# The second half's last five transposed column pairs computed as seven products for eight

## The chip, the cores and the metric

The kernel runs on one core of a Trainium2 chip. The metric is the device time of one execution in microseconds. Before the change it is 1893.95 us, the median of 3 runs (1892.88 to 1894.11).

## What is computed

One layer of a streaming encoder on 2048 prompt frames and 64 sample frames of width 1024:

```
h = rmsnorm(x, norm_g) @ w_in                  # 1024 -> 6144 columns
qa, ka, va, za, qb, kb, vb, zb, ga, gb = split(h)
oa = differential attention of qa, ka, va      # block-causal, 4 heads
ob = retention of qb, kb, vb                   # chunks of 64 frames, 4 heads
m  = sigmoid(ga) * ((norm(oa) * silu(za)) @ w_o_diff) + sigmoid(gb) * ((norm(ob) * silu(zb)) @ w_o_ret)
y  = x + m @ w_out
```

The outputs also hold the keys, the values and the retention state.

## The kernel before, in words

**Precision.** Every fp32 operand of a large product is split into two fp32r parts, high and low, and a product takes three matmuls: high by high, high by low, low by high. So each product appears in the profile as `xh,wh`, `xl,wh`, `xh,wl` (or with the weights first).

**Halves.** The frames are worked in two halves: frames 0 to 1023, and frames 1024 to 2047 with the 64 sample frames, 1088 in all. In each half the columns of `w_in` come as wide blocks of 512 (va, ka, qa, vb, by `natural`), which need row layout, and as 16 pairs of 2 x 128 columns (qb, kb, za, zb: two pairs each; ga, gb: four each), which are wanted transposed, columns on the partitions and frames on the free dimension.

**The 16 pairs of half 0** use a scheme of Strassen's kind (`strassen`, matmuls on L889): the 1024 inner columns are cut in two, the 256 output columns in two and the frames in two, and 7 products of sums of such blocks stand for the 8 plain products. The sums of the weights are made by POOL in `sum_prep` (operands b11, b21, b22 are plain blocks, t1 to t4 are sums), the sums of x once for all pairs.

**The 16 pairs of half 1** use the plain product (`transposed`, L1329, matmuls in `mm_group`, L1039): for each of the two column halves, the frames come in groups of 512, 256 and 320, and a group is 8 inner blocks x 3 matmuls. ACT copies each group out of its bank (`fin_t`, L1356 and L1358) into an `ev` buffer, from which it is stored to DRAM (zaT, zbT, gaT, gbT). The weights come by DMA (`ws`), ACT makes the high part (`wh`, L993) and POOL the low one (`wl`, L1003).

**Order.** An event loop in Python (`loop`) runs tasks by priority with a cost model and so writes the order of PE, ACT and DVE, which is kept as written. The order of SP, which issues all DMAs, and of POOL is made by the framework's scheduler. The attention over a half (`attn_head`, scores on L1577 and L1578, transposes on L1689, values on L1667 to L1669) and the retention run in one stream of tasks, `z_stream`; the products of the columns in another, `w_stream`, of lower priority, which fills PE while attention waits for the softmax. For the second half attention starts in the last group of the first transposed pair of half 1 and ends before the last pairs, so the last stretch of `w_stream` is pure products. Then `out_stream` reads za, zb, ga, gb and the attention results back (`z`, `on`, `ga`, `gb`), multiplies by w_o (`m_tile`, L2367 to L2369, 264 frames at a time) and by w_out (`y_quad`, L2491 to L2493).

A DMA on SP waits until the one issued eight before it has landed; SP works its list strictly in order.

## Time and profile before

| what | us |
|---|---|
| median of the runs | 1893.95 |
| the profiled execution | 1895.42 |
| its span in the profile | 1893.5 |
| PE busy | 1878.8 (99%) |
| DVE busy | 1267.1 (67%) |
| ACT busy | 955.2 (50%) |
| POOL busy | 586.2 (31%) |

The profiled execution is 1.9 us longer than its span, the time before the first and after the last instruction. The digits by slices of the profile's page are for 40 slices of 47.3 us. PE's busy time of a group of matmuls sums their durations, which overlap, since a matmul starts before the one ahead has ended; what a matmul costs is the distance from its start to the next start, read from the timeline. The waits of PE add up to under 10 us.

### The profile page before, as it was taken

How to read it: one execution, taken by the hardware profiler on the slowest of the kernel's cores; microseconds unless marked ns; L12 is line 12 of the kernel's file. 1: busy time of each engine (PE TensorE's matmuls, PEld its weight loads, DVE VectorE, ACT ScalarE, POOL GpSimd, SP SyncE). 2: the span in 40 equal slices, each digit the busy share in tenths (PEclk: the TensorE clock that was granted, in tenths of full speed). 3: DMA queues.
4: the chain of work that ended last, by engine and by line, in shares of the span. 5: the costliest groups of instructions: out<-in, count | busy, mean ns of one | idle time of the engine just before them, and what ended most of it. 6: DMA issues, size and time to landing. Idle time of an engine off the chain costs nothing.

```text
span 1893.5 us, 32104 instructions
## 1 busy us (share of the span) xinstructions
PE 1878.8 (99%) x10970; PEld 1649.9 (87%) x10970; DVE 1267.1 (67%) x2994; ACT 955.2 (50%) x2217; POOL 586.2 (31%) x557
## 2 busy tenths in 40 slices
PE   9999999999999999999999999999999999999999
PEld 7788888888888789888888899999999999999887
DVE  6765856657565667877577567668685339977664
ACT  6444654454434566465556454555565536654221
POOL 2420355555643132031211301211202535512442
PEclk9999999999999999999999999999999999999999
DMA  7664555565666885464524633643512758876542
GB/s 255 213 175 124 168 166 169 173 185 182 180 181 180 239 230 159 137 207 131 162 72 112 187 99 114 154 115 94 139 55 74 230 173 263 270 235 211 168 156 78
DMA packets 360581, 313.01 MB, mean 165 GB/s; under 512 B 67937, under 2 KB 310241, under 8 KB 360418
## 3 DMA queue, kind: packets, MB, share of 16 engines
q1 hardware_dynamic: 360418, 310.97, 55.8%
q8 instruction: 86, 1.41, 0.3%
q14 instruction: 77, 0.63, 0.1%
HBM read 205.43 MB, written 104.60 MB: 164 GB/s over the span
## 4 chain that ended last, share of the span: by engine, by line
PE 65%; DMA 1%; DVE 1%; SPq 1%; ACT 0%; issue 0%; ACTq 0%; POOL 0%; DVEq 0%; POOLq 0%
PE mm L1039 27%; PE at L1689 3%; PE s L1577 2%; PE s L1578 2%; PE pv L1669 2%; PE pv L1668 2%; PE pv L1667 2%; PE s L2491 1%; PE s L2493 1%; PE s L2492 1%; PE at L2368 1%; PE s L2368 1%; PE mm L2367 1%; PE s L2367 1%; PE at L2367 1%; PE s L2369 1%
## 5 line engine op out<-in xcount | busy, mean ns | idle before, releaser
L1003 POOL TENSOR_TENSOR wl<-ws,wh 128x512 fp32r<-128x512 f32 x125 | 167.7, 1355 | 384.3 <-ACT wh L993 309.8
L1039 PE MATMUL mm<-xh,wh 128*128 128x256 f32 (+2 forms) x784 | 259.7, 331 | 0.0
L1039 PE MATMUL mm<-xh,wl 128*128 128x256 f32 (+2 forms) x784 | 254.4, 325 | 1.5 <-POOL wl L1003 1.5
L1039 PE MATMUL mm<-xl,wh 128*128 128x256 f32 (+2 forms) x784 | 254.2, 324 | 0.0
L1039 PE MATMUL mm<-wh,xh 128*128 128x512 f32 x504 | 203.6, 404 | 0.0
L1039 PE MATMUL mm<-wh,xl 128*128 128x512 f32 x504 | 198.3, 393 | 0.0
L1039 PE MATMUL mm<-wl,xh 128*128 128x512 f32 x504 | 197.9, 393 | 0.0
L1617 ACT ACTIVATE row<-row,a_mx 128x1024 f32<-128x1024 f32 (+7 forms) x144 | 149.8, 1043 | 19.6 <-DVE a_mx L1596 19.5
L1039 PEld LDWEIGHTS mm<-xh,wl 128*128 128x128 f32 x784 | 148.0, 189 | 11.9 <-POOL wl L1003 1.9
L1039 PEld LDWEIGHTS mm<-xl,wh 128*128 128x128 f32 x784 | 148.4, 189 | 9.8
L1039 PEld LDWEIGHTS mm<-xh,wh 128*128 128x128 f32 x784 | 148.2, 189 | 10.0
L1705 DVE TENSOR_TENSOR atl<-at,ath 128x512 fp32r<-128x512 f32 (+1 forms) x144 | 92.8, 659 | 90.4 <-ACT ath L1703 90.1
L1703 ACT CAST ath<-at 128x512 fp32r<-128x512 f32 (+1 forms) x144 | 79.4, 565 | 116.6 <-PE at L1689 111.3
L1448 POOL TENSOR_TENSOR r_y<-r_y,r_sq 128x256 f32<-128x256 f32 x32 | 30.1, 941 | 340.6 <-DVE r_sq L1445 160.1
L1586 DVE CUSTOM_DVE_ANT_0 row<-s,dfar 128x512 f32<-128x512 f32 (+2 forms) x146 | 90.5, 634 | 60.2 <-PE s L1578 55.6
L768 POOL TENSOR_TENSOR wl<-ws,wh 128x256 fp32r<-128x256 f32 x64 | 57.8, 903 | 196.0 <-ACT wh L759 190.8
L1039 PEld LDWEIGHTS mm<-wh,xl 128*128 128x128 f32 x504 | 94.8, 188 | 21.4
L1039 PEld LDWEIGHTS mm<-wh,xh 128*128 128x128 f32 x504 | 95.1, 189 | 17.3 <-DVE raw L1211 0.2
L1039 PEld LDWEIGHTS mm<-wl,xh 128*128 128x128 f32 x504 | 95.2, 189 | 17.0
L1639 DVE SCALAR_TENSOR_TENSOR row<-row,a_w 128x1024 f32<-128x1024 f32 (+5 forms) x88 | 98.1, 1124 | 0.0
L1577 PE MATMUL s<-K,q 128*128 128x512 f32 (+3 forms) x244 | 91.6, 378 | 0.4 <-DVE a_acc L1586 0.2
L993 ACT CAST wh<-ws 128x512 fp32r<-128x512 f32 x128 | 77.5, 621 | 28.2 <-DMA ws<-in_w_in_dram 16.3
(497 smaller groups left out, 5442.0 us busy)
## 6 DMA issues: line engine op xcount, KB each, us to landing
ws<-in_w_in_dram SPq DMA_DIRECT2D x160, 256.0 KB, 3.4
q<-qT SPq DMA_DIRECT2D x128, 128.0 KB, 3.5
K<-kT SPq DMA_DIRECT2D x48, 256.0 KB, 4.2
V<-vN SPq DMA_DIRECT2D x24, 512.0 KB, 5.2
row<-in_x_prompt_dram SPq DMA_DIRECT2D x16, 512.0 KB, 4.3
wz<-in_w_in_dram SPq DMA_DIRECT2D x32, 256.0 KB, 4.0
row<-in_cache_k_T_dram SPq DMA_DIRECT2D x32, 256.0 KB, 3.6
row<-in_cache_v_diff_dram SPq DMA_DIRECT2D x32, 256.0 KB, 3.2
```

Source lines behind the costliest of these rows:

```text
L768: nc.gpsimd.tensor_sub(l[:, cs], src, h[:, cs].bitcast(F32))
L993: self.nc.scalar.copy(h, st)
L1003: self.nc.gpsimd.tensor_sub(l, st, h.bitcast(F32))
L1039: nc.tensor.matmul(ps, p, q, start=c == 0 and i == 0, stop=c == KC - 1 and i == 2)
L1577: nc.tensor.matmul(ps, q1s, kk, start=True, stop=False)
L1586: nc.vector.tensor_tensor_reduce(out=row[:, k0:k0 + n], in0=ps, in1=tab, scale=-SLOPES[h], scalar=3.0e38, op0=ALU.add, op1=ALU.min, accum_ ...
L1617: nc.scalar.activation(u, u, AF.Exp, bias=mx, scale=-1.0, accum_out=lp[:, k:k + 1])
L1639: nc.vector.scalar_tensor_tensor(out=u0, in0=u1, scalar=w[:, 0:1], in1=u0, op0=ALU.mult, op1=ALU.add)
L1689: nc.tensor.transpose(at[:, w:w + 128], src, self.ident)
L1703: nc.scalar.copy(ah[:, :w], at[:, :w])
L1705: nc.vector.tensor_sub(al[:, :w], at[:, :w], ah[:, :w].bitcast(F32))
L2367: nc.tensor.matmul(ps, wh[:, u, csl], oh, start=kt == 0, stop=False)
```

## The change

The first 11 pairs of half 1 stay plain products, with the frames in groups of 512, 288 and 288 (the 64 sample frames are split in two times 32). The last 5 pairs (the last of ga and all four of gb) go to a new function `quad`: 7 products of sums for 8, in the order of `PHASES`, product by product over all 5 pairs. A product of one pair is a group of 256 and a group of 288 frames, each of 4 inner blocks x 3 matmuls (L1547).

- **x operands.** The seven x operands (three plain blocks, four sums) are written to DRAM (`xd`) after the natural blocks of half 1: 12 stores of plain blocks straight from the x tiles, and 20 chunks of sums, each 8 adds on POOL, a cast on ACT, a subtraction on DVE and two stores (`x_again`, `x_chunk`). `x_pass` reads each phase's operand back, 2 x 1.114 MB (128 x 2176, high and low), into one of two slots in the x tile of the second 576 frames, after the last plain pair has read it.
- **Weight operands.** In half 0, `sum_keep` stores the sums t1 to t4 of the last 5 pairs to DRAM (`wsum`, 20 stores of 256 KB); in half 1, each product of a pair loads one 128 x 4 x 128 operand, from `wsum` or from `w_in`. Between load and matmul stand the cast on ACT and the subtraction on POOL or DVE (`next_low`).
- **Evacuation.** The banks of `quad` are added to running sums by DVE (`q_scaled`), with an ACT copy for two products of the seven; finished blocks go to `ev` and are stored in pieces of 128 x 256, and the sample frames 128 x 4 x 8.
- **Attention.** `attn_head` waits for its head's keys only; `at_pv` waits for the values.
- The x tiles of half 1 are laid out by block of frames, the weight sum t4 is formed earlier in the pair.

```diff
+PLAIN = 11
+PHASES = [("t2", "S2", "q_p6"), ("b11", "A11", "q_p1"), ("b21", "A12", "q_p2"), ("t1", "S1", "q_p5"),
+          ("t3", "S3", "q_p7"), ("t4", "A22", "q_p4"), ("b22", "S4", "q_p3")]
+NAMES = ("S1", "S3", "S2", "S4", "A11", "A12", "A22")
+WIDTH = (256, 288)
...
+        else:
+            for name, *_ in PHASES:
+                k = ("t1", "t2", "t4", "t3", "b11", "b21", "b22").index(name)
+                for c in c0:
+                    if k < 4:
+                        src = self.wsum[self.wpair[c], k // 2, :, :, 128 * (k % 2):128 * (k % 2) + 128]
+                    else:
+                        r0, n0 = ((0, 0), (512, 0), (512, 128))[k - 4]
+                        src = w[r0:r0 + 512, c + n0:c + n0 + 128].rearrange("(c p) n -> p c n", p=128)
+                    yield [128, 4, 128], src
...
+    def next_low(self, st, h, l, t, new, kind):
+        yield t - LAT
+        eng, cost = self.lighter() if kind == "quad" else (self.nc.gpsimd, self.G)
+        eng.tensor_sub(l, st, h.bitcast(F32))
+        t = cost(512, t)
+        self.give("ws", t)
...
+    def sum_keep(self, pair, i, k, raw, left, t):
+        yield t
+        b1, b2, tt = raw[i][0]
+        src = b1 if k else tt
+        t = self.st(self.wsum[pair, k, :, 2 * i:2 * i + 2, :], src, 1 << 18)
+        self.sum_free(raw, left, t)
...
-    def transposed(self, half, dst, d0, scale=None, grouped=True):
+    def transposed(self, dst, d0, scale, grouped):
         us = []
-        groups = [(0, 0, 512), (1, 0, 256), (1, 256, 320)]
+        groups = [(0, slice(0, 2), 512), (1, 0, 288), (1, 1, 288)]
         order = [(ct, k) for ct in range(2) for k in range(3)]
-        if self.npart[half] == 0:
-            groups = [(0, 0, 256), (0, 256, 256), (1, 0, 256), (1, 256, 320)]
+        if not self.nplain:
+            groups = [(0, 0, 256), (0, 1, 256), (1, 0, 288), (1, 1, 288)]
             order = [(0, 0), (1, 0), (0, 1), (1, 1), (0, 2), (0, 3), (1, 2), (1, 3)]
-        self.npart[half] += 1
...
+    def x_chunk(self, g, c, raw, a, n):
+
+        nc = self.nc
+        xh, xl = self.xnext[g]
+        for k, (b, j) in enumerate(((1, 1), (1, 0), (0, 0), (0, 1))):
+            h, l = (x[:, b, 4 * j + c, a:a + n].bitcast(F32) for x in (xh, xl))
+            nc.gpsimd.tensor_add(raw[:, k], h, l)
+            t = self.G(n, self.pe)
...
+    def x_again(self):
+
+        nc = self.nc
+        yield lambda: "nat1" in self.done
+        self.kept = 0
+        for g, w in enumerate(WIDTH):
+            gsl = slice(256 * g, 256 * g + w)
+            for k, (b, j) in (("A11", (0, 0)), ("A12", (0, 1)), ("A22", (1, 1))):
+                for x, d in zip(self.xnext[g], self.xd):
+                    self.kept = self.st(d[:, NAMES.index(k), :, gsl], x[:, b, 4 * j:4 * j + 4, :].bitcast(F32), 600000)
+                    yield self.pe + 4000
...
+    def x_pass(self):
+        self.xslots, self.xfree, self.parked = [], [(0, 0.0), (1, 0.0)], -1
+        yield lambda: self.parked == 1 and self.seg1_done is not None
+        yield max(self.seg1_done, self.kept)
+        for _, name, _ in PHASES:
+            s = yield from self.ring(self.xfree)
+            for x, d in zip(self.x_slot(s), self.xd):
+                t = self.ld(x.bitcast(F32), d[:, NAMES.index(name)].rearrange("p c t -> p (c t)"), 1114112)
                 yield self.pe
...
+    def quad(self, pairs):
+
+        nc = self.nc
+        self.u_room()
+        q = [[{"n": n, "g": g} for g, n in enumerate(WIDTH)] for _ in pairs]
+        for _, name, fin in PHASES:
+            yield lambda: len(self.xslots) > 0
+            s, tx = self.xslots.pop(0)
+            xs = [x.rearrange("p (c t) -> p c t", c=4) for x in self.x_slot(s)]
+            for i, pair in enumerate(pairs):
+                yield lambda: len(self.wq) > 0 and self.wq[0][2]
+                wh, wl, tw, tags, _ = self.wq.pop(0)
+                for g, n in enumerate(WIDTH):
+                    bank = yield from self.either(1, "mm", *(("tp",) if self.wo is None else ("s", "at")))
+                    ps = self.psum(bank)[:, :n]
+                    if max(tx, tw) > self.pe:
+                        yield max(tx, tw)
+                    for c in range(4):
+                        xh, xl = (x[:, c, 256 * g:256 * g + n] for x in xs)
+                        for k, (w, x) in enumerate(((wh, xh), (wh, xl), (wl, xh))):
+                            nc.tensor.matmul(ps, w[:, c], x, start=c == 0 and k == 0, stop=c == 3 and k == 2)
+                            t = self.P(n)
+                        if c == 1:
+                            yield self.pe
+                    self.spawn(getattr(self, fin)(q[i][g], ps, bank, t, *pair), 0, "w")
+                    if g == 0:
+                        yield self.pe
+                for tag in tags:
+                    self.give(tag, t)
+                yield self.pe
+            self.xfree.append((s, t))
+
+    def q_new(self, q):
+        return (yield from self.ring(self.ufree[q["g"]]))
...
+    def q_scaled(self, out, ps, add, scale, n, t):
+        if scale is None:
+            self.nc.vector.tensor_add(out, ps, add)
+        else:
+            self.nc.vector.scalar_tensor_tensor(out=out, in0=ps, scalar=scale, in1=add, op0=ALU.mult, op1=ALU.add)
+        return self.V(n, t)
...
+    def q_end(self, q, ps, bank, k, t, dst, b, scale, grouped):
+        ev = yield from self.q_ev(q["n"])
+        yield t
+        t = self.q_scaled(ev, ps, q[k], scale, q["n"], t)
+        self.give(bank, t)
+        yield t
+        self.q_put(q, dst, ev, b, grouped)
+        return t
...
-        ks, vs, tk, tv = self.heads.pop(0)
-        yield tk
+        hd = self.heads.pop(0)
+        ks = hd["ks"]
+        yield hd["tk"]
...
-        arows = pair["rows"]
-        yield max(pair["t"], tv)
+        yield lambda: pair["n"] == 2 and hd["tv"] is not None
+        arows, vs = pair["rows"], hd["vs"]
+        yield max(pair["t"], hd["tv"])
...
+        plain = [(c0, lambda half, a=a: self.transposed(*a), False) for c0, a in again[:PLAIN]]
+        c0s, args = zip(*again[PLAIN:])
+        seqs = [first + early + seq, [plain[0], wide[0], plain[1], wide[1], plain[2], wide[2], m0, m1, plain[3],
+                                      *later, (None, "nat"), (None, "ret"), *plain[4:],
+                                      (c0s, lambda half: self.quad(args), "quad")]]
```

The matmuls of L1039 in half 1's pairs are 784 of each of the three kinds: 288 of 256 columns, 256 of 320 and 240 of 512. After the change the first 11 pairs have 544 of each kind (32 of 256, 352 of 288, 160 of 512) and `quad` has 280 (140 of 256 and 140 of 288), 824 in all.

**PE in the pairs of half 1.** In before, in the last pair, at the border between the groups of 512 and 256 columns (L1039 of before is L1131 in the change, L1577 and L1578 are L1862 and L1863; `mm` is a bank of PSUM, `xh`/`xl` the parts of x, `wh`/`wl` those of the weights):

```order
L1039 MATMUL mm<-xh_6021,wh 128x512
L1039 MATMUL mm<-xl_6022,wh 128x512
L1039 MATMUL mm<-xh_6021,wl 128x512
L1039 MATMUL mm<-xh_6086,wh 128x256
L1039 MATMUL mm<-xl_6087,wh 128x256
L1039 MATMUL mm<-xh_6086,wl 128x256
L1039 MATMUL mm<-xh_6086,wh 128x256
L1039 MATMUL mm<-xl_6087,wh 128x256
```

and in the change, in `quad`, at the border between the groups of 288 and 256 columns:

```order
L1547 MATMUL mm<-xh_123,wh 128x288
L1547 MATMUL mm<-xl_124,wh 128x288
L1547 MATMUL mm<-xh_123,wl 128x288
L1547 MATMUL mm<-xh_123,wh 128x256
L1547 MATMUL mm<-xl_124,wh 128x256
L1547 MATMUL mm<-xh_123,wl 128x256
L1547 MATMUL mm<-xh_123,wh 128x256
L1547 MATMUL mm<-xl_124,wh 128x256
L1547 MATMUL mm<-xh_123,wl 128x256
L1862 MATMUL s<-K,q 128x384
```

A group is 12 matmuls in the place of 24, and no group of `quad` has 512 columns; between groups there stand scores of the attention (`K`, `q`) as long as it runs.

**SP at the start of the second attention.** In before (`K`, `q`, `V` are the attention's operands, `dnear` a table that it needs first, `qbT<-ev` the first transposed pair's stores, `xkeep` the sample frames of x):

```order
L271 DMA gbT<-ev 128x2x256
L271 DMA qbT<-ev 128x256
L271 DMA gbT<-ev 128x2x256
L271 DMA qbT<-ev 128x256 x2
L266 DMA dnear<-in_c_dnear_dram 128x512
L266 DMA K<-kT_59 64x1024
L266 DMA K<-kT_60 64x1024
L266 DMA K<-kT_59 64x1024
L266 DMA K<-kT_60 64x1024
L266 DMA q<-qT_57 64x2x256 x2
L266 DMA q<-qT_58 64x2x256 x2
```

and in the change:

```order
L284 DMA xd_77<-xl_122 128x4x256
L284 DMA gbT<-ev 128x2x256
L284 DMA xd_76<-xh_121 128x4x256
L284 DMA xd_77<-xl_122 128x4x256
L284 DMA qbT<-ev 128x256
L279 DMA dnear<-in_c_dnear_dram 128x512
L279 DMA K<-kT_59 64x1024
L279 DMA K<-kT_60 64x1024
L279 DMA K<-kT_59 64x1024
L279 DMA K<-kT_60 64x1024
L279 DMA q<-qT_57 64x2x256 x2
L279 DMA q<-qT_58 64x2x256 x2
```

The keys now follow stores of x blocks of 512 KB (four in all, three of them shown) and one store of the first pair, where they followed three stores of the first pair. Of the first pair 57 matmuls are still to come at the first score, where there were 9.

**SP in the last phases of `quad`.** In the change, about the loads of the seventh operand (`xh<-xd`, `xl<-xd`), with the stores of finished blocks and the loads of `w_o` (`wst`):

```order
L279 DMA xh_123<-xd_76 128x2176
L284 DMA gbT<-ev 128x4x8
L284 DMA gbT<-ev 128x256
L279 DMA xl_124<-xd_77 128x2176
L284 DMA gbT<-ev 128x256
L279 DMA wst<-in_w_o_diff_dram 128x2x256
L279 DMA ws<-in_w_in_dram 128x4x128
L284 DMA gbT<-ev 128x4x8
L284 DMA gbT<-ev 128x256
L284 DMA gaT<-ev 128x256
L284 DMA gaT<-ev 128x4x8
L284 DMA gaT<-ev 128x256
```

In before, in the last two pairs (`ws` are the weights, two of 256 columns to a row; `z`, `on` what the output stage reads first):

```order
L266 DMA ws<-in_w_in_dram 128x2x256
L266 DMA wst<-in_w_o_ret_dram 128x2x256
L266 DMA ws<-in_w_in_dram 128x2x256
L266 DMA wst<-in_w_o_diff_dram 128x2x256 x2
L271 DMA gbT<-ev 128x2x256
L266 DMA wst<-in_w_o_ret_dram 128x2x256 x2
L271 DMA gbT<-ev 128x256
L266 DMA wst<-in_w_o_diff_dram 128x2x256 x2
L266 DMA wst<-in_w_o_ret_dram 128x2x256 x2
L271 DMA gbT<-ev 128x256
L271 DMA gbT<-ev 1024x1x8
L266 DMA z<-zbT 128x2x264
```

The operands of x stand among the stores and the weights, on the one queue, and the loads of `w_o` behind them.

383 lines of the change are left out of this document (270 added, 113 removed).

## The prediction

> **What bounds the kernel now.** I read the page's busy shares and the chain first, then windows of the stretches that the change touches, then PE's timeline in them.
>
> ```profile
> PE 1878.8 (99%) x10970; PEld 1649.9 (87%) x10970; DVE 1267.1 (67%) x2994; ACT 955.2 (50%) x2217; POOL 586.2 (31%) x557
> ...
> PE 65%; DMA 1%; DVE 1%; SPq 1%; ACT 0%; issue 0%; ACTq 0%; POOL 0%; DVEq 0%; POOLq 0%
> ```
>
> PE is busy for 99% of the span and carries 65% of the chain that ended last; DVE, the next, has 67%. So the bound is PE's own work nearly everywhere, and a matmul fewer shortens the span if its operands come in time. Next, windows around the second attention's start, in its middle, and in the last pairs and the output stage (columns: window, length, busy time of PE, PEld, DVE, ACT, POOL with counts, granted clock, DMA share, GB/s):
>
> ```profile
> 560.00:585.00 25.00, 25.00 (x110) 20.38 (x109) 21.44 (x37) 12.27 (x24) 10.00 (x8) 1.00 0.59 170
> 600.00:620.00 20.00, 16.17 (x101) 14.47 (x99) 5.99 (x27) 7.86 (x22) 4.92 (x4) 1.00 1.06 271
> 620.00:635.00 15.00, 14.93 (x73) 12.83 (x74) 8.62 (x33) 5.44 (x14) 0.16 (x1) 0.89 1.04 259
> 635.00:800.00 165.00, 163.38 (x1035) 145.78 (x1035) 121.89 (x370) 98.51 (x250) 30.61 (x26) 1.00 0.64 184
> 1250.00:1400.00 150.00, 150.00 (x971) 138.04 (x970) 115.43 (x338) 89.63 (x183) 23.15 (x17) 1.00 0.37 100
> 1475.00:1500.00 25.00, 25.00 (x155) 23.08 (x155) 12.13 (x12) 14.38 (x27) 14.74 (x10) 1.00 0.69 195
> 1500.00:1520.00 20.00, 18.48 (x109) 16.52 (x108) 8.03 (x8) 9.62 (x18) 11.83 (x9) 1.00 0.90 263
> 1560.00:1580.00 20.00, 20.00 (x168) 20.00 (x167) 18.91 (x33) 11.55 (x32) 10.57 (x11) 1.00 0.90 276
> 1600.00:1650.00 50.00, 50.00 (x414) 50.00 (x413) 45.47 (x82) 33.30 (x85) 27.91 (x25) 1.00 0.90 277
> ```
>
> PE loses something at two places. About 600 to 635 it waits while the DMA share is 1.06 and 1.04, that is, full; and in 1500 to 1520 it misses 1.52 us with a share of 0.90. These are the two places where the change puts more transfers. PE's timeline names both losses:
>
> ```profile
> 607.90 0.22 PE L1577 MATMUL s<-K,q 128*128 128x128 f32 x1
> 610.75 0.41 PE L1578 MATMUL s<-K,q 128*128 128x384 f32 x1 [0.77 <-DMA q<-qT]
> ...
> 619.11 0.36 PE L1577 MATMUL tp<-K,q 128*128 128x256 f32 x1 [2.37 <-DMA q<-qT]
> ...
> 1519.40 0.50 PE L1039 MATMUL mm<-xh,wl 128*128 128x512 f32 x1 [1.52 <-POOL wl L1003]
> ```
>
> The first two are `q` loads that came late, 0.77 and 2.37 us, and behind them the granted clock falls to 0.89 over 15 us, which costs 15 x 0.11 = 1.65 us. The third is a late low part of a weight.
>
> **PE's work.** A matmul's price is its distance to the next start. Six rows give it: the first starts of three successive groups of 24 matmuls and of the group behind them, and two rows of 264 columns that stand seven steps apart.
>
> ```profile
> 1490.80 0.39 PE L1039 MATMUL mm<-xh,wh 128*128 128x512 f32 x1
> 1496.26 0.28 PE L1039 MATMUL mm<-xh,wh 128*128 128x256 f32 x1
> 1499.14 0.31 PE L1039 MATMUL mm<-xh,wh 128*128 128x320 f32 x1
> 1502.66 0.39 PE L1039 MATMUL mm<-xh,wh 128*128 128x512 f32 x1
> ...
> 1641.75 0.29 PE L2368 MATMUL pv<-ogl,w_o_reth 128*128 128x264 f32 x1
> 1642.61 0.28 PE L2369 MATMUL tp<-ogh,w_o_retl 128*128 128x264 f32 x1
> ```
>
> 512 columns: (1496.26 - 1490.80)/24 = 227.5 ns; 256: 2.88/24 = 120.0 ns; 320: 3.52/24 = 146.7 ns; 264: 0.86/7 = 123 ns. The change's 288 columns do not occur in before. The bounds are the neighbours, 123 and 147; the line from 256 to 320 gives 133.3, and it gives 123.3 at 264, where 123 was measured, so I take 133.3.
>
> Before, the 16 pairs are 3 x (288, 256, 240) matmuls of 256, 320 and 512 columns: 864 x 120.0 + 768 x 146.7 + 720 x 227.5 = 103.7 + 112.7 + 163.8 = 380.2 us. After, with `quad`: 3 x (32 + 140) = 516 of 256, 3 x (352 + 140) = 1476 of 288, 3 x 160 = 480 of 512: 61.9 + 196.8 + 109.2 = 367.9 us. That is **12.3 us less**, nearly all from `quad`. At the ends for 288 columns it would be 27 us less or 7.5 us more (1476 x 13.4 = 19.8).
>
> The Trainium skill, page "TensorE: Matmul & The Clock Gate", section "Back-to-back issue gap", speaks against this change: it gives a sustained 81 ns a matmul at 128 columns and 131 ns at 512. An estimate by that line (98, 102, 106 and 131 ns at 256, 288, 320 and 512) makes 260.1 us of the old work and 263.6 of the new, a loss of 3.5 us, because there are 120 more matmuls. The rows above differ: 227.5 ns at 512 against 120.0 at 256, so columns are paid here, and the measurement decides.
>
> **The second attention's start.** SP's timeline of before:
>
> ```profile
> 596.07 0.33 SPq L266 DMA_DIRECT2D dnear<-in_c_dnear_dram  x1
> 596.45 2.40 SPq L266 DMA_DIRECT2D K<-kT  x4
> 598.90 2.55 SPq L266 DMA_DIRECT2D q<-qT  x4
> ```
>
> The keys are issued at 596.45 and the first scores run at 607.9. In the change the scores stand 48 matmuls earlier in the pair (57 left against 9), 48 x 133 = 6.4 us, and groups of plain matmuls stand between them, which would cover the two `q` waits. But four stores of 512 KB (2.1 MB, 7.7 us at 271 GB/s) now stand ahead of the keys on SP, and eight more (4.6 MB, 17 us at that rate) follow between the loads of `q`, `K` and `V`, in the very stretch that was full. The ends: all of 0.77 + 2.37 + 1.65 = 4.8 us is won, or the keys come 7.7 us late and PE, whose order is fixed, waits for all of it. These are about equally far, and the cover and the queue oppose each other; I take 0.
>
> **Between.** The sums of x cost POOL 160 adds, at most 836 ns each by the row below (128 x 256; these are half as wide or less), 134 us at the very most; POOL has 135 of 165 us free in 635 to 800 alone. DVE gets 20 subtractions of 689 ns, 14 us, and ACT 20 casts of 621 ns, 12 us, beside an attention that keeps DVE at 115.4 of 150 us. DVE also takes over the banks of `quad`: 70 adds of 419 to 689 ns, some 33 us, of which four of the seven phases lie partly beside attention. There a bank freed late is a wait of PE on DVE that before does not have. Ends 0 and 6 (one late bank of 0.4 us in every fifth of the 70); most lies under other filler, so I take **+1**. The stores of weight sums in half 0 (20 of 256 KB) hold the weight buffers of five pairs until they have landed, 3.4 us by the row of the stores of the same size below (KB each, median us to landing). The products of the pair ahead hide that, and in 560 to 585 PE has no gap at a DMA share of 0.59, so I take 0; with no cover at all it would be 5 x 3.4 = 17 us.
>
> ```profile
> L1003 POOL TENSOR_TENSOR wl<-ws,wh 128x512 fp32r<-128x512 f32 x125 | 167.7, 1355 | 384.3 <-ACT wh L993 309.8 <-PE mm L1035 33.7 <-DMA obT<-row 20.2
> L768 POOL TENSOR_TENSOR wl<-wz,wh 128x256 fp32r<-128x256 f32 x64 | 53.5, 836 | 0.0
> L1705 DVE TENSOR_TENSOR atl<-at,ath 128x512 fp32r<-128x512 f32 x112 | 75.6, 689 | 71.7 <-ACT ath L1703 71.6
> L1442 DVE TENSOR_TENSOR r_sq<-tp,r_sq 128x256 f32<-128x256 f32 x32 | 13.4, 419 | 14.2 <-ACT r_sq L1434 14.1
> L993 ACT CAST wh<-ws 128x512 fp32r<-128x512 f32 x128 | 77.5, 621 | 28.2 <-DMA ws<-in_w_in_dram 16.3 <-PE mm L1039 5.2 <-PE tp L889 2.2
> ```
>
> ```profile
> gbT<-ev SPq DMA_DIRECT2D x24, 256.0 KB, 3.4
> ```
>
> **The last phases.** A phase of `quad` takes PE 5 x 12 x (120.0 + 133.3) = 15.2 us, three of them 45.6 us. Attention is over before the last three, so nothing else fills PE. By the order of SP, from the load that follows phase four to the first load of `ga` stand: four x operands of 1.114 MB, 7 weight operands, 45 stores of finished blocks (30 of 128 KB), 12 loads of `w_o` and 14 of `z` and `on`: 4.5 + 1.8 + 4.2 + 3.1 + 3.8 = 17.4 MB. Up to the last load of `w_o` but one, which the end of `quad` and the first tiles of the output stage need, it is 14.0 MB. The highest rate of any window above is 277 GB/s. At that rate 14.0 MB take 50.5 us, 4.9 more than PE's 45.6; 17.4 MB take 62.8, 17.2 more. The ends are 0 (the loads of phase four and the first `w_o` go ahead of time, as in 1475 to 1500 at 195 GB/s without a wait) and 17.2. I take **+5**, by the highest rate seen, since the `z` and `on` that follow are for later tiles. Weights come in time: a cast of 621 ns and a subtraction of 1355 ns at most stand against 3.04 us of PE per pair and phase.
>
> The Trainium skill, page "DMA: Bandwidth & Descriptors", section "Specifications", gives an HBM limit of about 358 GB/s per core. An estimate by it moves the 14.0 MB in 39.1 us and the 17.4 MB in 48.6, so that this term would be 0 to 3 us; no window here shows more than 277 GB/s, and that is what I use.
>
> **Sum.** -12.3 + 0 + 1 + 0 + 5 = -6.3 us against the profiled execution, 1895.4 (span 1893.5 and 1.9 around it), so 1889.1. The median of the runs shown is 1.5 below that execution, so the forecast is **1887.6**.
>
> **Rivals**, each against the median of 1893.95.
> - *The queue decides the end (slower).* All 17.4 MB must pass before the output stage runs freely: 17.2 in place of 5. -12.3 + 1 + 17.2 = +5.9, **1899.9**. It decides from the rate at which 17.4 MB take more than 45.6 + 11.3 = 56.9 us, below 306 GB/s. For it: one queue in order, the 1.52 us wait of before at a share of 0.90. Against: 1600 to 1650 runs at 277 GB/s with PE busy for all 50 us, and the slots are loaded one phase ahead.
> - *Attention starts free.* The matmuls between the scores cover the late `q` and the clock stays up, and the last phases wait for nothing: -12.3 - 4.8 + 1 = -16.1, **1877.9**. For it the 48 matmuls; against it the 6.7 MB in the full stretch.
> - *Attention starts late.* The stores ahead of the keys cost their 7.7 us: -12.3 + 7.7 + 1 + 5 = +1.4, **1895.4**, no change that shows. For it the share of 1.06.
> - *The change saves no PE time.* The price goes by the matmul more than by the column, and 288 columns cost what 320 do: +7.5 + 6 = +13.5, **1907.5**. The straight line through three measured widths is against it. The Trainium skill's page on TensorE named above goes this way, as an estimate, with its flat line.
>
> **How the numbers follow.** Forecast 0.47, of which 0.10 lies within 0.2% (3.8 us, about what can be told from no change here); queue 0.20 (0.15 slower); free start 0.15, all faster; late start 0.15 (0.08 same, 0.04 slower, 0.03 faster); no saving 0.03. Faster 0.37 + 0.15 + 0.03 = 0.55, same 0.10 + 0.05 + 0.08 = 0.23, slower 0.15 + 0.04 + 0.03 = 0.22. The forecast's own range is 1882 to 1893 (last phases from 0 to 10 late). The range is 1877 to 1903: it takes in the free start and the queue with 3 us of its spread, and leaves out the far ends of 288 columns and of the keys.
>
> **What would show it.** On PE, 288 columns at 133 ns in the timeline; if 147, the first step is wrong. About 600 to 620, the `q` rows: waits of some 3 us if the term is 0, none for the free start, waits on `K` or `q` of 8 us for the late one. In the last 46 us of `quad` there would be PE waits of about 5 us, on `xh` or `xl` from `xd`, on `ev` through DVE, or on `w_o` at the output's start; 17 us for the queue, with the DMA share at 0.9 and more. Waits of PE on DVE in the first phases beyond 1 us would make the middle term wrong, and a wait in half 0 on the weights that of `wsum`.

## The result and the profile after

The changed kernel takes **1915.45 us** (median of 4 runs, 1914.33 to 1916.72), before 1894.01: a ratio of 1.0112 with a 95% interval of 1.0099 to 1.0124, so 21.4 us slower. The forecast of 1887.6 and its range up to 1903 missed it. The profiled execution of after took 1916.72 us with a span of 1914.9.

The busy shares and the chain's engines, from the page of after:

```profile
PE 1879.6 (98%) x11090; PEld 1652.8 (86%) x11090; DVE 1327.4 (69%) x3089; ACT 965.8 (50%) x2242; POOL 667.3 (35%) x727
...
PE 58%; DMA 5%; DVE 4%; POOL 1%; issue 1%; SPq 1%; ACT 1%; DVEq 0%; POOLq 0%; ACTq 0%
```

PE is as busy as before, 1879.6 us for 1878.8, with 120 matmuls more. But its share of the chain fell from 65% to 58%, and DMA's and DVE's rose from 1% to 5% and 4%: there are now waits in the path that end in a transfer. The windows (columns as in the prediction) say where:

```profile
600.00:620.00 20.00, 13.37 (x79) 12.71 (x79) 6.46 (x34) 5.63 (x20) 0.00 (x0) 0.83 0.95 260
620.00:635.00 15.00, 14.99 (x96) 13.26 (x94) 11.58 (x36) 9.95 (x23) 5.13 (x4) 1.00 1.00 238
1250.00:1400.00 150.00, 146.27 (x967) 134.48 (x966) 113.50 (x321) 87.24 (x181) 23.51 (x25) 0.99 0.57 156
1475.00:1500.00 25.00, 25.00 (x206) 24.98 (x205) 12.55 (x28) 9.03 (x18) 9.36 (x8) 1.00 0.68 214
1500.00:1520.00 20.00, 19.80 (x158) 19.59 (x157) 11.69 (x22) 8.47 (x14) 10.01 (x7) 1.00 0.99 309
1520.00:1540.00 20.00, 15.11 (x101) 14.61 (x101) 7.69 (x18) 2.35 (x4) 2.58 (x2) 0.83 0.87 254
1540.00:1560.00 20.00, 15.84 (x108) 14.96 (x107) 16.23 (x25) 9.86 (x17) 7.74 (x6) 0.92 0.87 244
1600.00:1650.00 50.00, 50.00 (x415) 50.00 (x414) 45.27 (x78) 31.61 (x81) 27.10 (x24) 1.00 0.90 275
```

Three stretches lose: 600 to 620 (6.6 us idle and a clock of 0.83), 1250 to 1400 (3.7 idle, none before) and 1520 to 1560 (9.1 idle, clocks of 0.83 and 0.92). The output stage is unchanged. The list of PE's waits (line, what was waited for, us in total, times, longest) names waits in each of the three:

```profile
PE mm L1131 <- ACT ev L1574: 5.8, 1, 5.8
PE s L1547 <- DVE ev L1567: 4.9, 2, 3.2
PE pv L1952 <- ACT ath L1988: 3.4, 1, 3.4
PE s L1547 <- DVE wl L741: 2.5, 1, 2.5
```

To add up work and losses alike in all kernels I give each matmul a fixed **price** by its columns, near the medians of the traces: 109, 119.3, 121.3, 133, 146.7 and 230.4 ns at 128, 256, 264, 288, 320 and 512 (the few of 384 columns at about 175, the few of 64 and 2 at about 109). What lies between one start and the next beyond that price is a **loss**: a wait, or a stretch at a lower clock. PE's whole time is then price plus losses, here by stretch of the one profiled execution of each kernel (us; a stretch slightly below zero is priced slightly too high):

| | price | to 500 | 500–700 | 700–1050 | 1050–1300 | 1300–1500 | 1500–1580 | to the end | sum |
|---|---|---|---|---|---|---|---|---|---|
| before | 1863.0 | 10.4 | 10.6 | -0.3 | 2.5 | -0.4 | 1.8 | 0.9 | 1888.3 |
| after | 1849.8 | 10.7 | 13.9 | 4.1 | 13.3 | 1.6 | 14.7 | 1.7 | 1909.8 |

So the work fell by 13.2 us and the losses rose by 34.7.

**Near 600.** PE's, ACT's and SP's timelines of after (start, length, engine, line, operation, in brackets the idle time before it and what ended it):

```profile
600.49 0.29 PE L1131 MATMUL mm<-xh,wl 128*128 128x288 f32 x1
606.56 0.61 PE L1131 MATMUL mm<-xh,wh 128*128 128x288 f32 x1 [5.78 <-ACT ev L1574]
606.97 0.44 PE L1131 MATMUL mm<-xl,wh 128*128 128x288 f32 x1
607.21 0.44 PE L1131 MATMUL mm<-xh,wl 128*128 128x288 f32 x1
```

```profile
606.14 0.37 ACT L1574 COPY ev<-mm 128x256 f32<-128x256 f32 x1 [10.69 <-DMA qbT<-ev]
```

```profile
593.14 2.40 SPq L279 DMA_DIRECT2D K<-kT  x4
595.59 2.55 SPq L279 DMA_DIRECT2D q<-qT  x4
598.24 0.54 SPq L279 DMA_DIRECT2D ws<-in_w_in_dram  x1
598.82 3.12 SPq L279 DMA_DIRECT2D q<-qT  x4
602.04 0.54 SPq L284 DMA_DIRECT2D qbT<-ev  x1
...
604.92 2.84 SPq L284 DMA_DIRECT2D qbT<-ev  x1
```

The stores of the first plain pair (`qbT<-ev`) stand behind the keys and two sets of `q` on SP and leave at 602.04 and 604.92. Until then ACT has no staging buffer, its copy waits 10.69 us, the PSUM bank is not freed, and PE stops for 5.78. Behind it two successive starts lie 240 ns apart in place of 133: the granted clock is 0.50 from 604.4 to 611.2 us. The Trainium skill, page "TensorE: Matmul & The Clock Gate", section "Part 1: The HAM clock gate", says that the clock goes to one half after an idle window of some 3.4 us; the wait of 5.78 us and the 240 ns agree. So a wait of this length costs more than itself.

**In the middle of attention.** ACT's timeline, then PE's:

```profile
1254.66 0.58 ACT L1988 CAST ath<-at 128x512 fp32r<-128x512 f32 x1 [4.17 <-PE at L1974]
1260.44 0.51 ACT L1492 CAST xsh<-xsl 128x384 fp32r<-128x384 f32 x1 [5.20 <-DMA xd<-xsh]
1260.86 1.06 ACT L1988 CAST ath<-at 128x512 fp32r<-128x512 f32 x2
```

```profile
1261.49 0.39 PE L1952 MATMUL pv<-ath,V 128*128 128x256 f32 x1 [3.44 <-ACT ath L1988]
```

The cast of an x sum (`xsh`) has one buffer. It waits 5.20 us until the store of the last sum has landed, and the cast that attention needs stands behind it in ACT's order. This happened once; with the halved clock behind it (3.4 us at 0.50) it makes some 5.3 of the 13.3 us lost from 1050 to 1300. The next largest, 1.75 us, comes the same way by POOL, whose adds for a sum (`xsl`), late by a wait for a store, stand from 1092 to 1100 ahead of retention's `r_y`:

```profile
1100.05 0.73 POOL L1728 TENSOR_TENSOR r_y<-r_y,r_sq 128x256 f32<-128x256 f32 x1
1100.81 1.47 DVE L1731 SCALAR_TENSOR_TENSOR r_o<-r_o,gsub,r_y 128x256 f32<-128x256 f32 x1 [2.12 <-POOL r_y L1728]
1102.94 0.38 PE L1954 MATMUL pv<-atl,V 128*128 128x256 f32 x1 [1.75 <-DVE atl L1990]
```

**In the last phases.** DVE's, then PE's timeline:

```profile
1528.03 0.42 DVE L1567 TENSOR_TENSOR ev<-s,u 128x256 f32<-128x256 f32 x1 [5.73 <-DMA gbT<-ev]
1532.07 0.46 DVE L1567 TENSOR_TENSOR ev<-s,u 128x288 f32<-128x288 f32 x1 [3.61 <-DMA gbT<-ev]
```

```profile
1528.60 0.36 PE L1547 MATMUL s<-xh,wh 128*128 128x256 f32 x1 [3.17 <-DVE ev L1567]
1532.58 0.61 PE L1547 MATMUL s<-xh,wh 128*128 128x288 f32 x1 [1.72 <-DVE ev L1567]
1543.50 0.39 PE L1547 MATMUL s<-xh,wl 128*128 128x256 f32 x1 [0.90 <-POOL wl L741]
```

It is the same chain: a store that has not landed holds a staging buffer, the buffer holds DVE, DVE holds the bank, the bank holds PE. From 1490 to 1570 the stores to `gaT` and `gbT` took 3.6 us at the median and up to 8.6 to land, with loads of 1.1 MB between them. Of the 9.1 us idle from 1520 to 1560, 4.9 end on `ev` by this chain and 4.2 on parts of the weights (`wl` 2.5 and 0.9, `wh` 0.8). Two rows of transfers (over the whole kernel; KB each, median us to landing):

```profile
xh<-xd SPq DMA_DIRECT2D x7, 1088.0 KB, 7.8
gbT<-ev SPq DMA_DIRECT2D x32, 128.0 KB, 3.1
```

### The profile page after: what moved, and what is told of

It reads as the page before. It is cut to its first block, busy times and chain, and to the rows that moved or that the text cites. A ratio compares the mean times of both kernels' runs of the same rounds, so it can differ in the third digit from the quotient of the medians.

```text
span 1914.9 us, 32977 instructions
## 1 busy us (share of the span) xinstructions
PE 1879.6 (98%) x11090; PEld 1652.8 (86%) x11090; DVE 1327.4 (69%) x3089; ACT 965.8 (50%) x2242; POOL 667.3 (35%) x727
## 4 chain that ended last, share of the span: by engine, by line
PE 58%; DMA 5%; DVE 4%; POOL 1%; issue 1%; SPq 1%; ACT 1%; DVEq 0%; POOLq 0%; ACTq 0%
PE mm L1131 19%; PE at L1974 3%; PE s L1863 2%; PE s L1862 2%; PE mm L1547 2%; PE pv L1954 2%; PE pv L1953 2%; PE pv L1952 2%; DMA gbT<-ev 1%; PE s L2776 1%; PE s L2778 1%; PE s L2777 1%; DMA gaT<-ev 1%; DMA xd<-xsl 1%; PE at L2653 1%
## 5 line engine op out<-in xcount | busy, mean ns | idle before, releaser
L741 POOL TENSOR_TENSOR wl<-ws,wh 128x512 fp32r<-128x512 f32 x106 | 140.9, 1340 | 291.6 <-ACT wh L726 204.8
L1131 PE MATMUL mm<-wh,xh 128*128 128x512 f32 x504 | 203.5, 404 | 0.0
L1131 PE MATMUL mm<-wl,xh 128*128 128x512 f32 x504 | 198.0, 393 | 1.1 <-POOL wl L741 1.1
L1131 PE MATMUL mm<-wh,xl 128*128 128x512 f32 x504 | 198.2, 393 | 0.0
L1131 PE MATMUL mm<-xh,wh 128*128 128x288 f32 (+2 forms) x544 | 180.3, 332 | 5.8 <-ACT ev L1574 5.8
L1131 PE MATMUL mm<-xh,wl 128*128 128x288 f32 (+2 forms) x544 | 176.4, 324 | 0.0
L1131 PE MATMUL mm<-xl,wh 128*128 128x288 f32 (+2 forms) x544 | 176.3, 324 | 0.0
L1131 PEld LDWEIGHTS mm<-xh,wh 128*128 128x128 f32 x544 | 103.0, 189 | 12.8 <-ACT ev L1574 6.0
L1131 PEld LDWEIGHTS mm<-wh,xl 128*128 128x128 f32 x504 | 94.6, 188 | 21.6
L1131 PEld LDWEIGHTS mm<-wl,xh 128*128 128x128 f32 x504 | 95.0, 189 | 19.2 <-POOL wl L741 1.9
L1131 PEld LDWEIGHTS mm<-wh,xh 128*128 128x128 f32 x504 | 94.8, 188 | 17.6 <-DVE raw L1302 0.2
L1131 PEld LDWEIGHTS mm<-xh,wl 128*128 128x128 f32 x544 | 103.0, 189 | 7.0 <-POOL wl L741 0.3
L1131 PEld LDWEIGHTS mm<-xl,wh 128*128 128x128 f32 x544 | 103.2, 190 | 6.5
L1862 PE MATMUL s<-K,q 128*128 128x512 f32 (+3 forms) x246 | 93.1, 380 | 0.3 <-DVE a_acc L1871 0.2
L1863 PE MATMUL s<-K,q 128*128 128x512 f32 (+3 forms) x246 | 89.7, 365 | 0.0
```

What stands on the lines that cost most here:

```text
L741: eng.tensor_sub(l, st, h.bitcast(F32))
L1131: nc.tensor.matmul(ps, p, q, start=c == 0 and i == 0, stop=c == KC - 1 and i == 2)
L1862: nc.tensor.matmul(ps, q1s, kk, start=True, stop=False)
L1863: nc.tensor.matmul(ps, q2s, kk, start=False, stop=True)
```

## The experiments

Times are medians; the ratio is to before, with its 95% interval.

**All pairs plain, the rest of the change kept.**

```diff
-PLAIN = 11
+PLAIN = 16
...
-                                     (c0s, lambda half: self.quad(args), "quad")]]
...
-                    self.spawn(self.x_pass(), 0, "w")
-                    self.spawn(self.x_again(), 1, "w")
```

> All 16 pairs of half 1 as plain products: no quad, no stores or loads of x operands, no weight sums kept; the rest of the change stays (groups of 512, 288 and 288, attention waiting for its keys alone, t4 earlier). PE's own work is then 96 x 120 + 1536 x 133 + 720 x 229 = 381 us in these pairs, as before. Theory A, all 32 us of new losses come from the added transfers and the buffers they hold: 1891 to 1896 us, and no wait of PE near 600 us above the 3 us of before. Theory B, the new grouping and the earlier keys and queries are to blame at the start of attention (the first pair's stores queue behind them): the 5.8 us wait of PE on the copy to ev stays, and the time is 1897 us or more.

Measured: 1904.76, 1.0052 [1.0037, 1.0067]. Without one sum of x, without its transfers and without the products, the kernel is still 10.7 us slower than before. The waits near 600 are there all the same:

```profile
PE mm L1131 <- ACT ev L1574: 5.7, 1, 5.7
PE mm L1131 <- POOL wl L741: 2.7, 3, 1.6
...
PE tp L1334 <- DVE raw L1319: 1.3, 2, 1.0
```

If the two parts simply add, half of the 21 us is not the sums' doing but that of what was rewritten around them.

**The x sums' buffers freed later in the planner's book**, so that it sets the next cast behind a store that has landed.

```diff
-                    self.give(tag, self.kept)
+                    self.give(tag, self.kept + 8000)
```

> The change, but the buffers of a chunk of x sums count as free 8 us later in the scheduler's book, so the next chunk's cast is placed later in ACT's fixed order. Theory A1, ACT stood behind a cast that waited for a store to land (5.2 us at 1255, PE 3.4 us and the clock halved for 3.4 us more): some 6 to 8 us less between 1050 and 1300, total 1907 to 1910. Theory A2, these waits only show a full DMA: they move elsewhere, 1913 to 1917.

Measured: 1907.23, 1.0069 [1.0054, 1.0084], 8.2 us less than after. The loss from 1050 to 1300 falls from 13.3 to 2.2 us, and in the window that lost 3.73 us only 1.32 are idle:

```profile
1250.00:1400.00 150.00, 148.68 (x1006) 138.08 (x1006) 123.50 (x346) 94.65 (x199) 51.60 (x83) 1.00 0.64 173
```

The edit touches nothing but the time at which these buffers count as free, and PE's two waits shown above, behind ACT's cast and behind POOL's adds, are gone with it. So the sums' wait for a buffer, with other work queued behind it in a fixed order, is shown as a cause.

**Seven staging buffers in the last phases.** Four more of 288 columns come from the pool of sums.

```diff
+        more = pool.tile([128, 1152], F32, tag="u3", name="u3")
+        self.evs = [(more[:, 288 * k:288 * k + 288], 0.0) for k in range(4)]
...
-        ev = yield from self.q_ev(q["n"])
+        buf = yield from self.ring(self.evs)
```

> The change, but quad has 7 staging buffers for finished blocks instead of 3. Theory C1, in the last two phases DVE waits for a staging buffer whose store takes up to 8.6 us to land, though the DMA engines are not full (share 0.87): the phases fall from 22 to about 16 us each, 10 to 12 us less with the halved clock, total 1903 to 1906. Theory C2, the rate of the DMA engines bounds the last phases: less than 3 us, the wait goes to the weights or the x operands, 1913 to 1916.

Measured: 1911.77, 1.0095 [1.0078, 1.0112], 3.7 us less. The loss from 1500 to 1580 falls from 14.7 to 7.9 in the profiled execution; that one took 1909.06, the shortest of its four, and after's 1916.72, the longest of its four, so the 6.8 us are more than the medians show. The last three windows of it:

```profile
1500.00:1520.00 20.00, 20.00 (x162) 20.00 (x161) 15.23 (x31) 9.11 (x15) 11.73 (x8) 1.00 1.08 334
1520.00:1540.00 20.00, 18.85 (x150) 18.64 (x149) 12.74 (x23) 6.59 (x11) 4.28 (x3) 1.00 1.02 303
1540.00:1560.00 20.00, 17.13 (x124) 16.70 (x124) 7.26 (x14) 6.87 (x11) 9.19 (x8) 0.91 1.00 285
```

With buffers to spare the transfers run at 334, 303 and 285 GB/s for 309, 254 and 244, the share is full, and the wait moves to the weights (`wh`, 2.5 us). So the buffers bind first; that the rate binds behind them fits the full share and was not tested by itself.

**The twelve direct stores of x on ACT's queue**, to clear SP from 579 to 640.

```diff
-                    self.kept = self.st(d[:, NAMES.index(k), :, gsl], x[:, b, 4 * j:4 * j + 4, :].bitcast(F32), 600000)
+                    nc.scalar.dma_start(d[:, NAMES.index(k), :, gsl], x[:, b, 4 * j:4 * j + 4, :].bitcast(F32))
```

> The change, but the 12 direct stores of x blocks are issued by ACT, whose order is kept as written, so they go out when the natural blocks are done (about 940 us) and not between 579 and 640 on SP. Theory D1, these stores fill the queue and the engines at the start of attention and delay the first pair's stores and the queries: the wait of 5.8 us near 600 falls to 0 to 2 us, the clock stays up, 4 to 8 us less, total 1907 to 1911. Theory D2, the wait there comes of the order of keys, queries and the first pair's stores on SP: it stays within 1 us, 1913 to 1917.

Measured: 1914.12, 1.0103 [1.0088, 1.0118]: no difference from after that can be told. The stores now go out from 1047 to 1168, PE still waits 6.4 us near 600, and so the stores of x ahead of the keys, the cost that the prediction feared most there, are not the cause of that loss.

**Before, with attention waiting for the keys alone.**

```diff
-        self.heads.append((ks, vs, tk, tv))
+            self.heads.append((ks, vs, hd))
...
+        hd["tv"] = tv
```

> The kernel before, with one part of the change alone: attention waits for its head's keys, the values are waited for later. The order of SP at the start of attention is the same as in before. If the 11 us that the change costs without quad came from this rule: 1900 us or more. If they come from the place of the last block of half 0, as E is to test: within 2 us of 1894.

Measured: 1894.32, 0.9999 [0.9989, 1.0008]. This part of the change neither costs nor gains by itself.

**All pairs plain, and the fourth split of x held back** until the last blocks of the first half are out, which gives SP before's order at the second attention's start.

```diff
+            if p == 3:
+                yield lambda: self.nout == 4
```

> All 16 pairs plain, as in the first experiment, and the last four splits of x wait until the last block of half 0 has been copied out, as the order of DVE was in before. Theory E, in the change this block comes out behind all splits, its store to gbT stands on SP behind keys and queries and holds one of three staging buffers for 16 us, so that the first pair's copies, and by its full banks PE, wait 5.7 us and the clock halves: the wait near 600 goes and the time is 1894 to 1898. Rival F, the groups of 512, 288 and 288 with two more stores for the sample frames fill the staging buffers by themselves: still 1902 or more.

Measured: 1906.45, 1.0065 [1.0050, 1.0080]. The wait on `ev` near 600 is gone and the loss from 500 to 700 falls from 14.9 to 10.4 us, below before's 10.6: on SP stores of the first pair now go out at 592.47, ahead of the keys at 596.24, and that order was its cause. But 700 to 1050 loses 8.9 for 5.2, and the time is no better: a gain in one stretch came back as waits on DVE in the next.

**The three edits together** (later buffers, seven staging buffers, the split held back).

```diff
+                    self.give(tag, self.kept + 8000)
...
+        buf = yield from self.ring(self.evs)
...
+                yield lambda: self.nout == 4
```

> The change with quad, with the later freeing of the chunks' buffers, the 7 staging buffers and the order of the last splits together. If the three losses are apart from each other, 1915.5 - 8.2 - 3.7 - 8 = 1895.5, 1892 to 1899; if what one gives another takes back in a full DMA, 1900 or more.

Measured: 1906.37, 1.0066 [1.0049, 1.0082]. The gains don't add: 9.1 us in all.

**The same with six pairs as sums.**

```diff
-PLAIN = 11
+PLAIN = 10
```

> As the kernel with the three mends, but with 6 pairs in quad instead of 5. One more pair saves PE 23.9 - 21.3 = 2.6 us, and a phase lasts 18.2 us of PE for the same 2.23 MB of x. If the transfers of x bound the last phases: 3 to 6 us below the kernel with 5 pairs; if the stores of the finished blocks and the weights do, which grow with the pairs: 1 to 3 us below, or none.

Measured: 1923.91, 1.0157 [1.0141, 1.0173], 17.5 us more, which neither expectation held. A loss of 16.0 us appears between 1300 and 1400, beside a price that is only 2.6 lower: PE waits there on DVE in attention and retention (2.37 us on `atl`, 1.74 on `r_hi` and shorter ones), with the clock halved twice; why is not shown. From 1500 us to the end the loss is some 3 us larger than with five pairs, so a sixth pair did not ease the last phases either.

**All pairs plain: which rewritten part costs?** Four runs, each with a part as in before. First the column groups, 512, 256 and 320 for 512, 288 and 288:

```diff
-        groups = [(0, slice(0, 2), 512), (1, 0, 288), (1, 1, 288)]
+        groups = [(0, (0, 1), 512), (1, 0, 256), (1, 1, 320)]
```

> All 16 pairs plain (as in the run that gave 1904.8 us) and, in the second half, the column groups of before again: 512, 256 and 320 columns for 512, 288 and 288, the operands of x in before's layout, the sample columns in one store a pair for two. Theory F (the reorganisation's 11 us come from one part, and it is this one: smaller stores in larger number on SP's queue, 32 columns apart): 1894 to 1898. Theory G (no part carries it: the planner writes another order of DVE, ACT and SP wherever anything is changed, and every order but before's has some waits of 1 to 6 us more): within 3 us of 1904.8, with the excess over the matmuls' own price spread over at least three places between 500 and 1100 us.

Then the weight pieces:

```diff
-        self.spawn(self.next_low(st, h, l, t, new, kind), 0, "w")
-        yield self.act - PACE
+        self.nc.gpsimd.tensor_sub(l, st, h.bitcast(F32))
```

> All 16 pairs plain, and the second half's weight pieces taken as in before: POOL's subtraction is queued at once behind ACT's copy, not later by a task of its own. Theory H (the later subtraction is the cause: PE waits on POOL's wl 2.7 us in 3 waits there, 1.5 us in before, and each also brings a stretch at half the clock where it is over 3 us): 1899 to 1901, and the waits on wl between 600 and 1000 us are gone. Theory G: within 3 us of 1904.8.

Then `t4`'s old place and the old pacing:

```diff
-            if name == "b21":
+            if name == "t4":
...
-            yield t2 - LAT - PACE
+            yield self.dve - PACE
```

> All 16 pairs plain, the first half's last difference of weights (t4) formed at its old place, and the score tasks paced by DVE's book again as in before. Theory I (t4 at the earlier place holds POOL in the first half: 64 rows of POOL stand earlier there, and the excess of the first 550 us rose from 10 to 13 us): 1901 to 1902, with the first half's excess back at 10. Theory G: within 3 us of 1904.8.

And all three at once:

```diff
-        groups = [(0, slice(0, 2), 512), (1, 0, 288), (1, 1, 288)]
+        groups = [(0, (0, 1), 512), (1, 0, 256), (1, 1, 320)]
...
+        self.nc.gpsimd.tensor_sub(l, st, h.bitcast(F32))
...
+            if name == "t4":
```

> All 16 pairs plain and all three undone together: column groups, weight pieces, t4 and pacing as in before; what is left of the change is the keys alone for attention, the pools' new bounds and the order of the marks. If the parts add up (F, H, I): 1892 to 1897. Theory G: not at before's time, 1898 to 1908, since DVE's and ACT's order still agrees with before's in about half of the rows only.

Measured: 1897.66, 1.0020 [1.0011, 1.0030] with the groups; 1902.08, 1.0045 [1.0028, 1.0062] with the weights; 1901.40, 1.0039 [1.0024, 1.0053] with `t4` and pacing; 1896.48, 1.0012 [1.0003, 1.0022] with all three. So 8.3 of the 10.7 us come from these parts, 7.1 with the groups alone. Only the groups are clear by themselves: the 2.7 and 3.4 us of the other two leave intervals that overlap with that of the plain version, and the 1.2 us that all three give beyond the groups are not clear either. PE's list with the groups undone begins so:

```profile
PE mm L1130 <- ACT ev L1571: 6.8, 1, 6.8
PE at L588 <- DVE epst L3110: 1.1, 1, 1.1
```

The wait near 600 is still there; the waits on `wl` and `raw` are down to 0.2 us each, and the loss from 700 to 1050 is -0.5 for 5.2 us.

**Groups or their stores?** Before's groups, with the sample columns in two stores a pair.

```diff
-                t = self.st(dst[:, T:TT], ev[:, npr:n], 1 << 16)
+                for b in range(2):
+                    t = self.st(dst[:, T + 32 * b:T + 32 * b + 32], ev[:, npr + 32 * b:npr + 32 * b + 32], 1 << 16)
```

> The run with before's column groups (all pairs plain, 1897.7 us), but with each pair's 64 sample columns stored by two stores of 32 columns again in place of one. Theory F1 (what the 288-column groups cost is their stores: 32 more places on SP's queue, 3,600 more packets under 512 B): 1902 to 1905. Theory F2 (it is the groups themselves, when their banks end and how ACT's copies fall among the attention's work): 1896 to 1899.

Measured: 1899.17, 1.0026 [1.0015, 1.0037], 1.5 us more than with one store, which the intervals do not tell apart. So it is not the stores. It is the groups, or what went back together with them: the layout of the x tiles and the loads of the sample columns, which no run tests apart.

**The changed kernel with before's groups in its 11 plain pairs.**

```diff
-        self.xnext = [[x.rearrange("p (b c t) -> p b c t", b=2, c=KC) for x in room] for room in self.xroom]
+        self.xnext = [[x.rearrange("p (c b t) -> p b c t", b=2, c=KC) for x in room] for room in self.xroom]
...
+        groups = [(0, (0, 1), 512), (1, 0, 256), (1, 1, 320)]
```

> The changed kernel, with the last 5 pairs as sums, but with before's column groups (512, 256, 320) and one store of sample columns in the 11 plain pairs; the sums read the same tiles as halves of 288 columns, with the sample columns in their middle. If the groups' cost is the one that showed with all pairs plain (7.1 us over 16 pairs, so 5 over 11): 1909 to 1912. If the gain there was another order by luck: 1913 to 1919.

Measured: 1912.35, 1.0094 [1.0078, 1.0109], 3.1 us less than after, between the two expectations. The loss from 700 to 1050 is down from 4.1 to 0.2 us, but 1500 to 1580 rises from 14.7 to 18.0: what is won ahead is in part lost again in the last phases.

**All that was found, mended at once**, with the 5 pairs as sums.

```diff
+                    self.give(tag, self.kept + 8000)
...
+        buf = yield from self.ring(self.evs)
...
+        groups = [(0, (0, 1), 512), (1, 0, 256), (1, 1, 320)]
...
+            if name == "t4":
```

> All that the runs found, mended at once in the changed kernel with its 5 pairs as sums: chunk buffers of the x sums come free 8 us later in the planner's book (-8.2 alone), a ring of 7 staging buffers in the last phases (-3.7 alone), before's column groups in the plain pairs, weight pieces, t4 and pacing as in before (-8.3 together with all pairs plain). If the losses add up: 1894 to 1898, so all of the 21 us is accounted for and no more than before's time is reached. If they overlap, as two of them did (8.2 and 3.7 gave 9.1 together): 1898 to 1903. If the last phases are bound by the rate of the transfers whatever stands ahead of them: PE's waits between 1500 and 1560 us remain over 8 us there.

Measured: 1899.23, 1.0027 [1.0017, 1.0037]: 16.2 of the 21.4 us are back, and before's time is not reached. It is the best version with the sums, so no version here beats before. Its price and losses beside those of the runs that bear on it (us):

| | price | to 500 | 500–700 | 700–1050 | 1050–1300 | 1300–1500 | 1500–1580 | to the end | sum |
|---|---|---|---|---|---|---|---|---|---|
| all plain | 1862.9 | 11.2 | 14.9 | 5.2 | 1.8 | -0.6 | 1.9 | 0.9 | 1898.0 |
| all plain, three parts undone | 1863.0 | 9.3 | 12.1 | 0.2 | 2.9 | 1.1 | 0.0 | 0.9 | 1889.3 |
| later buffers | 1849.8 | 10.4 | 14.3 | 4.2 | 2.2 | 2.0 | 15.6 | 2.1 | 1900.6 |
| seven staging buffers | 1849.8 | 11.6 | 13.0 | 5.0 | 11.4 | 1.6 | 7.9 | 1.7 | 1902.1 |
| all mended | 1849.8 | 9.6 | 11.6 | 1.9 | 3.8 | 0.2 | 13.3 | 2.2 | 1892.4 |

The last row against the second: the sums save 13.2 us of PE's price, and from 1500 to 1580 they lose 13.3. The windows there, PE's largest waits in the last phases and its two largest in the output stage, and DVE, PE and SP about the first of them:

```profile
1500.00:1520.00 20.00, 16.32 (x123) 15.79 (x123) 9.99 (x20) 7.29 (x13) 4.43 (x4) 0.93 0.98 281
1520.00:1540.00 20.00, 18.46 (x130) 18.02 (x130) 11.06 (x21) 8.05 (x13) 8.15 (x7) 0.90 1.03 282
```

```profile
PE at L1575 <- ACT wh L729: 4.5, 2, 3.1
PE at L2687 <- DVE ogl L2643: 2.1, 3, 0.9
PE s L2686 <- DVE ga L2699: 1.6, 1, 1.6
```

```profile
1508.85 5.67 SPq L279 DMA_DIRECT2D ws<-in_w_in_dram  x3
1515.34 0.46 DVE L1595 TENSOR_TENSOR ev<-at,u 128x288 f32<-128x288 f32 x1 [6.05 <-DMA gbT<-ev]
1517.83 0.58 PE L1575 MATMUL at<-xh,wh 128*128 128x256 f32 x1 [3.14 <-ACT wh L729]
```

The DMA share is full, at 281 and 282 GB/s. The weights that PE waits for were issued at 1508.85, behind the two loads of an x operand, and landed at 1517.06. ACT could not have cast them sooner either: the cast ahead of it waited 7.87 us for DVE, and DVE had stood 6.05 us at a staging buffer whose store had not landed. So the chain of after is still there with seven buffers, and this run does not tell it from the rate. The last product of a pair now starts at 1538.3, 1.6 us sooner than in before (1539.9). But the output stage then waits on DVE's `ogl` and `ga`, 4 us in all. That fits the order product by product, which finishes the gates of all five pairs together at the end, where the output stage needs them at once; no run tested it. The 6.8 us idle in 1500 to 1560 fall short of the over 8 that were set as the mark for a bound by the rate; with the halved clock behind the waits the loss is 13.3.

## Why the prediction was wrong

**PE's work: right.** Forecast 12.3 us less, measured 13.2 at the prices above (12.3 came from 227.5 ns at 512 columns, where the whole trace has 230.4). The median distance of 288 columns is 133 ns, as the line between 256 and 320 gave; the rival that saves no PE time is out. With it goes the flat line of the Trainium skill's page "TensorE: Matmul & The Clock Gate", section "Back-to-back issue gap".

**The second attention's start: 0 forecast, +3.3 measured** (500 to 700: 13.9 for 10.6). That is inside the bounds given, -4.8 to +7.7, but by another chain. The keys were not late and the waits on `q` fell from 3.8 us to 0.9 in all; in their place stand the stores of the first pair, queued behind the keys and `q`, and a staging buffer that they hold; with that order undone the wait was gone. The prediction asked what stands ahead of the keys, and not what stands behind them. Moving the stores of x away changed nothing.

**Between: +1 forecast, +15 measured** (700 to 1300: 17.4 for 2.2). This is the step that failed. The term of +1 priced the added adds and casts by the time that POOL, ACT and DVE have free ("most lies under other filler"). What cost was their wait for a buffer on an engine whose order is fixed: one cast stood 5.20 us at its only buffer with attention's cast queued behind it, and POOL's adds held up retention's `r_y`. The later buffers took 11.1 us of loss out of 1050 to 1300 and 8.2 out of the time. The 4.4 us in 700 to 1050 go with the column groups, which the prediction put at nothing without a reason: undone, that stretch loses 0.2.

**The stores of weight sums: right.** Forecast 0; the first 500 us lose 10.7 for 10.4.

**The last phases: +5 forecast, +12.9 measured.** The place was named, and so was the sign (`ev` through DVE), but the term was priced by the rate alone. 50.5 us for 45.6 of PE assumed a rate of 277 GB/s and buffers enough to hold it. Before's own trace has 303 GB/s from 9 to 29 us; at that rate the 14.0 MB take 46.2 us, and the term would have been 0.6. The first phase ran at 309 GB/s, and then the staging buffers bound before the rate did: the transfers fell to 254 and 244 GB/s while PE waited. Seven buffers brought 334 GB/s at first and halved the loss in the profiled execution. "Weights come in time" failed too: 4.2 us of PE's waits ended on them. The rival in which the queue decides the end had the right place and, at 17.2, the nearer price, but the staging buffers came before the rate.

**The sum.** -13.2 + 0.3 + 3.3 + 15.2 + 2.0 + 12.9 + 0.8 = +21.3 (to 500, 500–700, 700–1300, 1300–1500, 1500–1580, the rest, behind the price), which is what lies between the two profiled executions (1916.72 and 1895.42). One more thing was missing as a term at all: a rewrite of the part that lies around the change. The planner derives the order of every engine from its book, so a column group of another width moves DVE's and ACT's work for hundreds of us. With all pairs plain it cost 10.7 us by itself.

**Open.** Why 288 and 288 columns lead to more waits than 256 and 320 is not shown: price and stores are ruled out; left are the order that the planner writes for them and the layout of the x tiles, which changed with them. In the last phases it is not shown whether the rate binds once there are buffers enough: with all mended they still lose 13.3 us. Nor is it shown what the remaining 2.3 us of the plain version are; its wait on `ev` near 600, 6.1 us, is the largest thing that before does not have.

## What to carry to other kernels

Price an added operation by what it waits for and by what is queued behind it on its engine, not by the engine's free share: a single buffer whose release is a DMA's landing makes a 0.5 us cast into a 5 us stop. Where finished blocks leave through few staging buffers, ask what stands behind them on the queue as well as ahead, and work out the landing time of a small store among large loads. And before trusting a gain from less work, run the kernel with that work unchanged and only the rewritten surroundings: here these took 10.7 us, and a saving of 13 us in products was matched by 13 us in the stretch where their operands and results have to pass.

## What the hardware showed that was not expected

- Transfers reached 334 GB/s at a share of 1.08 over 20 us with seven staging buffers, and with before's groups in the plain pairs 345 GB/s from 1480 to 1500 us and 361 from 1483 to 1503, both at a share of 1.05. The Trainium skill, page "DMA: Bandwidth & Descriptors", section "Specifications", gives a limit of about 358 GB/s a core. The 361 stand at that limit. So neither the highest rate seen in some windows nor a full share says what a stretch can move: a share of 0.98 went with 281 GB/s in one run, 1.05 with 361 in another.
- From 1490 to 1570 us, beside loads of 1.1 MB, stores of 128 and 16 KB landed 3.6 us after issue at the median and up to 8.6; in before, the stores of `ev` from 1450 to 1545 took 3.0 and up to 6.2.
- The wait of 5.78 us left the clock at 0.50 from 604.4 to 611.2 us. PE ran for 4.6 us of that, at 240 ns for 133 a matmul, so some 2.3 us were lost on top of the wait. Shorter waits do it too: in the traces of all these runs, every wait of PE of 2.15 us or more ended in or was followed by at least 3.4 us at half clock, and of those from 1.3 to 2.02 us most were not. In before, 2.37 us were enough: the clock was 0.50 from 621.2 to 624.5, although PE had been busy for 1.39 us of the 3.4 ahead of it.
